# Huber loss over two 8192x8192 matrices: one run of numbers in tiles of 128x13248, four slots, in place of 128x8192 in six

## The chip, the core and the metric

The kernel runs on one core of a Trainium2 chip. The metric is device microseconds of one execution. Three runs of the kernel before took 1873.52, 1872.58 and 1871.90 us; the median, 1872.58, is its time.

## The reference

```python
def reference(pred, target):            # both 8192 x 8192, float32
    delta = 1.0
    diff = pred - target
    abs_diff = np.abs(diff)
    return np.where(abs_diff <= delta, 0.5 * diff**2, delta * (abs_diff - 0.5 * delta))
```

Every output element depends on one element of each input, so any cut of the matrices into tiles will do. The input is 2 x 268.4 MB, the output 268.4 MB: 805.3 MB have to be moved, whatever the order.

The kernels compute the loss as max(|d| - 0.5, 0.5 c^2), where d is the difference and c is d held between bounds. The kernel before holds |d| between 0 and 1; the kernel after holds d between -1 and 1. The square is the same.

## The kernel before

The 8192 rows are cut into 64 tiles of 128 rows by 8192 columns, 4 MB in float32, so a partition holds one row of 32 KB. Six slots of that size lie in on-chip memory. A tile takes two: its pred slot becomes the difference and then its absolute value, and its target slot becomes the clamped value, then the half square, then the output, which is stored from there.

For one tile there are five operations. VectorE subtracts (`sub`, L41), ScalarE takes the absolute value (`absolute`, L49), VectorE clamps (`clamp`, L44), ScalarE squares with a scale (`half_square`, L52), and VectorE adds -0.5 to the absolute value and takes the maximum with the half square (`finish`, L55). The order on each engine is the order in which the program is written, since the schedule is manual. `compute` emits the finish of a tile one tile later, between the subtract and the clamp of the next. The last four tiles are computed in four pieces of 2048 columns each.

All transfers are issued by SyncE (SP) on one queue, in program order. In round i, `load(i)` issues pred (L66) and target (L68) of tile i, then `store` issues the output (L73) of tile i-2. The slots are chosen by lists: `load` takes as the pred slot one whose tile is through with it (`spent`), and as the target slot one whose store has been issued (`free`). So three tiles are asked for before the first store, and a target load waits until the store out of its slot has landed. An SP instruction that waits holds back everything behind it on SP. The target load and the store of the last tile are cut into four pieces of 1 MB.

Of the kernel before, what the change touches and what calls it, by code (L numbers as in the profile page):

```python
# [1 line left out]

# [4 lines left out]


@with_exitstack
def kernel(  # L10
    ctx: ExitStack,
    tc: tile.TileContext,
    pred: bass.AP,
    target: bass.AP,
    out: bass.AP,
):
    nc = tc.nc
    P = 128
    fp32 = mybir.dt.float32
    Alu = mybir.AluOpType  # L20
    Act = mybir.ActivationFunctionType
    SQRT_HALF = 0.70710678118654752

    n_rows, W = pred.shape
    pred_t = pred.rearrange("(n p) m -> n p m", p=P)
    targ_t = target.rearrange("(n p) m -> n p m", p=P)
    out_t = out.rearrange("(n p) m -> n p m", p=P)
    n = pred_t.shape[0]

    NSLOT = 6  # L30
    PIECES = 4
    FINE = 4

    pool = ctx.enter_context(tc.tile_pool(name="slots", bufs=1))
    slots = [pool.tile([P, W], fp32, name=f"slot{k}") for k in range(NSLOT)]
    free = list(range(NSLOT))
    spent = []
    pending = []

    def sub(a, b):  # L40
        nc.vector.tensor_tensor(out=a, in0=a, in1=b, op=Alu.subtract)  # L41

    def clamp(a, b):
        nc.vector.tensor_scalar(  # L44
            out=b, in0=a, scalar1=0.0, scalar2=1.0, op0=Alu.max, op1=Alu.min
        )

    def absolute(a):
        nc.scalar.activation(out=a, in_=a, func=Act.Abs)  # L49

    def half_square(b):
        nc.scalar.activation(out=b, in_=b, func=Act.Square, scale=SQRT_HALF)  # L52

    def finish(a, b):
        nc.vector.scalar_tensor_tensor(  # L55
            out=b, in0=a, scalar=-0.5, in1=b, op0=Alu.add, op1=Alu.max
        )

    def cuts(pieces):
        w = W // pieces  # L60
        return [slice(k * w, (k + 1) * w) for k in range(pieces)]

    def load(i):
        ia = spent.pop(0) if i >= 3 else free.pop(0)
        ib = free.pop(0) if free else spent.pop(0)
        nc.sync.dma_start(out=slots[ia], in_=pred_t[i, :, :])  # L66
        for c in cuts(PIECES if i == n - 1 else 1):
            nc.sync.dma_start(out=slots[ib][:, c], in_=targ_t[i, :, c])  # L68
        return ia, ib

    def store(i, ib):
        for c in cuts(PIECES if i == n - 1 else 1):
            nc.sync.dma_start(out=out_t[i, :, c], in_=slots[ib][:, c])  # L73
        free.append(ib)

    ctx.enter_context(tc.manual_schedule())

    waiting = []

    def settle(keep):  # L80
        while len(waiting) > keep:
            finish(*waiting.pop(0))

    def compute(a, b, pieces):
        lag = 1 if pieces == 1 else 2
        if pieces > 1:
            while waiting and waiting[0][0].shape[1] == W:
                finish(*waiting.pop(0))
        for c in cuts(pieces):
            sub(a[:, c], b[:, c])  # L90
            absolute(a[:, c])
            settle(lag - 1)
            clamp(a[:, c], b[:, c])
            half_square(b[:, c])
            waiting.append((a[:, c], b[:, c]))

    for i in range(n):
        ia, ib = load(i)
        if i >= 2 and i < n - 1:
            store(*pending.pop(0))  # L100
        spent.append(ia)
        pending.append((i, ib))
        compute(slots[ia], slots[ib], PIECES if i >= n - FINE else 1)
    settle(0)
    for p in pending:
        store(*p)


# [1 line left out]
_INS = ['pred', 'target']  # L110
_OUTS = [((8192, 8192), 'float32')]


# [23 lines left out]
```

## Time and profile before

| | |
|---|---|
| median of three runs | 1872.58 us |
| the profiled execution, its own time | 1873.31 us |
| its span in the profile | 1871.5 us |
| VectorE (DVE) busy | 1386.8 us, 74%, 228 instructions |
| ScalarE (ACT) busy | 906.0 us, 48%, 153 instructions |
| moved | 805.36 MB, 430 GB/s over the span |
| loads and stores | 198 transfers on one queue |

The profile is of one execution. The span runs from the first to the last instruction; the execution's own time is 1.8 us longer. Busy shares are means over the span. The DMA row of the page gives, for 40 equal slices, the share of time in which the 16 DMA engines of the core hold a packet, in tenths. A view of windows gives, for each stretch of the span, the busy time and number of instructions of VectorE, ScalarE and GpSimd, then the granted TensorE clock (not used here, 1.00), the DMA share and the GB/s. SPq is SyncE's sequencer, which issues the transfers. "Time to landing" is from the issue of a transfer to the arrival of the last of its 16 completion marks, one from each DMA engine. In the chain of waits, each line gives the start and the duration of a piece, followed back from the last instruction of the program; the lines of a timeline give start, duration, engine, line, operation and shapes, and in brackets how long the engine had been idle and what ended that.

### The profile page before, as it was taken

To read this page: it belongs to the slowest core of one execution; us is meant where nothing else is said; L and a number is where in the kernel's file an instruction comes from. 1 tells how busy PE (TensorE), PEld (TensorE's weight loads), DVE (VectorE), ACT (ScalarE), POOL (GpSimd) and SP (SyncE) were. 2 spreads that over 40 slices of the span, in tenths; PEclk is the share of its full clock that TensorE was granted. 3 is DMA by queue.
4 is the path that set the end of the run, shared out by engine and by line. 5 is a ranking of instruction groups with operands and counts; after the bars stand their busy time and mean duration, and the time that the engine had idled before them with its cause. 6 is when DMAs were issued, how large, how long until landed. Compare 5 with 4: busy or idle time off the path is not lost.

```text
span 1871.5 us, 823 instructions
## 1 busy us (share of the span) xinstructions
DVE 1386.8 (74%) x228; ACT 906.0 (48%) x153; POOL 0.2 (0%) x4
## 2 busy tenths in 40 slices
DVE  3886776868678687686776867768678686686787
ACT  2644545444454444544545445444454444544555
POOL 0000000000000000000000000000000000000000
DMA  9999999999999999999999999999999999999998
GB/s 415 415 432 431 432 432 429 434 426 430 435 431 434 434 431 434 433 432 434 432 432 435 431 434 432 433 434 433 432 433 434 431 435 431 434 433 432 434 434 382
DMA packets 28517, 805.36 MB, mean 430 GB/s; under 512 B 3168, under 2 KB 3168, under 8 KB 3168
## 3 DMA queue, kind: packets, MB, share of 16 engines
q1 hardware_dynamic: 28512, 805.32, 100.0%
q14 instruction: 5, 0.04, 0.0%
HBM read 536.87 MB, written 268.44 MB: 430 GB/s over the span
## 4 chain that ended last, share of the span: by engine, by line
DMA 68%; DVE 31%; ACT 0%; issue 0%; DVEq 0%; SPq 0%
DMA out_dram<-slot 35%; DMA slot<-in_target_dram 32%; DVE slot L41 15%; DVE slot L55 15%; DVE slot L44 1%; ACT slot L49 0%; DVEq L132 0%; DVEq L41 0%; SPq L66 0%; SPq L68 0%; DVEq L44 0%; SPq L73 0%
## 5 line engine op out<-in xcount | busy, mean ns | idle before, releaser
L41 DVE TENSOR_TENSOR slot<-slot,slot 128x8192 f32<-128x8192 f32 (+1 forms) x76 | 558.1, 7343 | 456.2 <-DMA slot<-in_target_dram 456.2
L49 ACT ACTIVATE slot<-slot 128x8192 f32<-128x8192 f32 (+1 forms) x76 | 452.4, 5952 | 576.3 <-DVE slot L41 576.3
L52 ACT ACTIVATE slot<-slot 128x8192 f32<-128x8192 f32 (+1 forms) x76 | 452.3, 5951 | 375.7 <-DVE slot L44 375.7
L55 DVE SCALAR_TENSOR_TENSOR slot<-slot,slot 128x8192 f32<-128x8192 f32 (+1 forms) x76 | 557.5, 7337 | 7.1 <-ACT slot L52 7.1
L44 DVE TENSOR_SCALAR slot<-slot 128x8192 f32<-128x8192 f32 (+1 forms) x76 | 284.8, 3747 | 11.0 <-ACT slot L49 11.0
L49 ACT ACT_TABLE_LOAD x1 | 1.3, 1283 | 0.7 <-PEq L121 0.7
L121 POOL MEMSET const-bfloat16-1.0<- 128x1 bf16 x1 | 0.1, 101 | 0.0
L121 POOL MEMSET const-uint8-127<- 128x1 uint8 x1 | 0.1, 101 | 0.0
L121 POOL MEMSET const-float32-0.0<- 128x1 f32 x1 | 0.1, 98 | 0.2 <-issue 0.2
L121 POOL MEMSET const-float32-1.0<- 128x1 f32 x1 | 0.1, 98 | 0.0
## 6 DMA issues: line engine op xcount, KB each, us to landing
slot<-in_pred_dram SPq DMA_DIRECT2D x64, 4096.0 KB, 30.6
slot<-in_target_dram SPq DMA_DIRECT2D x63, 4096.0 KB, 19.3
out_dram<-slot SPq DMA_DIRECT2D x63, 4096.0 KB, 21.4
slot<-in_target_dram SPq DMA_DIRECT2D x4, 1024.0 KB, 15.2
out_dram<-slot SPq DMA_DIRECT2D x4, 1024.0 KB, 9.8
```

Of the source, the lines that this page charges most:

```text
L41: nc.vector.tensor_tensor(out=a, in0=a, in1=b, op=Alu.subtract)
L44: nc.vector.tensor_scalar(out=b, in0=a, scalar1=0.0, scalar2=1.0, op0=Alu.max, op1=Alu.min)
L49: nc.scalar.activation(out=a, in_=a, func=Act.Abs)
L52: nc.scalar.activation(out=b, in_=b, func=Act.Square, scale=SQRT_HALF)
L55: nc.vector.scalar_tensor_tensor(out=b, in0=a, scalar=-0.5, in1=b, op0=Alu.add, op1=Alu.max)
L121: nc = _bacc.Bacc("TRN2", target_bir_lowering=False, num_devices=1)
```

## The change

The two inputs and the output are each read as one run of 67,108,864 numbers. It is cut into 40 blocks: the first of 128x7616, the other 39 of 128x13248, so a partition holds 52,992 consecutive bytes and rows of the matrices no longer matter. There are four slots in place of six, two for pred (`a0`, `a1`) and two for target and output (`b0`, `b1`); tile i uses the pair i mod 2.

Two tiles are loaded ahead. Then each round computes tile i, stores it, and loads tile i+2. So on SP a store of tile i stands before both loads of tile i+2, and there are 138 transfers in all. Tiles 0 and 1 and the two before the last are loaded in halves, the last in quarters, with its first two pred quarters ahead of its first target quarter. The last store is in three quarters and two eighths.

A tile is computed in thirds of 4416 columns; the first in halves of 3808, the last but one in quarters of 3312 and the last in eighths of 1656. In each piece VectorE subtracts and clamps from -1 to 1, then ScalarE squares and takes the absolute value. The finish of a piece is emitted after the clamp of the third piece from it on; at the end of each tile the rest are emitted, so nothing of a tile is left for the next.

```diff
-    NSLOT = 6
-    PIECES = 4
-    FINE = 4
+    total = pred.shape[0] * pred.shape[1] // P
+    W = 13248
+    H, Q, E = W // 2, W // 4, W // 8
+    widths = [W] * (total // W)
+    if total % W:
+        widths.insert(0, total % W)
+    n = len(widths)
+    starts = [sum(widths[:i]) * P for i in range(n)]
+
+    def block(x, i):
+        flat = x.rearrange("r m -> (r m)")
+        return flat[starts[i] : starts[i] + P * widths[i]].rearrange("(p m) -> p m", p=P)
...
+    a_slots = [pool.tile([P, W], fp32, name=f"a{k}") for k in range(2)]
+    b_slots = [pool.tile([P, W], fp32, name=f"b{k}") for k in range(2)]
...
+    def load(i):
+        a, b = a_slots[i % 2], b_slots[i % 2]
+        def get(dst, src, c):
+            nc.sync.dma_start(out=dst[:, c], in_=block(src, i)[:, c])
+        if i == n - 1:
+            c = cuts([Q] * 4)
+            order = [(0, 0), (0, 1), (1, 0), (1, 1), (0, 2), (1, 2), (0, 3), (1, 3)]
+            for which, k in order:
+                get((a, b)[which], (pred, target)[which], c[k])
+            return
+        w = widths[i]
+        pieces = [w // 2] * 2 if i in (0, 1, n - 3, n - 2) else [w]
+        for c in cuts(pieces):
+            get(a, pred, c)
+            get(b, target, c)
+
+    def store(i):
+        pieces = [Q] * 3 + [E] * 2 if i == n - 1 else [widths[i]]
+        for c in cuts(pieces):
+            nc.sync.dma_start(out=block(out, i)[:, c], in_=b_slots[i % 2][:, c])
+
+    def compute(i):
+        if i == n - 1:
+            pieces = [E] * 8
+        elif i == n - 2:
+            pieces = [Q] * 4
+        elif i == 0:
+            pieces = [widths[0] // 2] * 2
+        else:
+            pieces = [W // 3] * 3
+        todo = []
+        def finish(keep):
+            while len(todo) > keep:
+                a, b = todo.pop(0)
+                nc.vector.scalar_tensor_tensor(                                # L86
+                    out=b, in0=a, scalar=-0.5, in1=b, op0=Alu.add, op1=Alu.max
+                )
+        for c in cuts(pieces):
+            a, b = a_slots[i % 2][:, c], b_slots[i % 2][:, c]
+            nc.vector.tensor_tensor(out=a, in0=a, in1=b, op=Alu.subtract)      # L92
+            nc.vector.tensor_scalar(                                           # L93
+                out=b, in0=a, scalar1=-1.0, scalar2=1.0, op0=Alu.max, op1=Alu.min
+            )
+            nc.scalar.activation(out=b, in_=b, func=Act.Square, scale=SQRT_HALF)
+            nc.scalar.activation(out=a, in_=a, func=Act.Abs)
+            todo.append((a, b))
+            finish(2)
+        finish(0)
...
-    for i in range(n):
-        ia, ib = load(i)
-        if i >= 2 and i < n - 1:
-            store(*pending.pop(0))
-        spent.append(ia)
-        pending.append((i, ib))
-        compute(slots[ia], slots[ib], PIECES if i >= n - FINE else 1)
-    settle(0)
-    for p in pending:
-        store(*p)
+    load(0)
+    load(1)
+    for i in range(n):
+        compute(i)
+        store(i)
+        if i + 2 < n:
+            load(i + 2)
```

More of the change, by code (lines that the diff above doesn't have):

```diff
@@ L22 @@
     SQRT_HALF = 0.70710678118654752
[L24 to L28, printed above, removed]
-    NSLOT = 6
-    PIECES = 4
-    FINE = 4
-    pool = ctx.enter_context(tc.tile_pool(name="slots", bufs=1))
[L35 to L57, printed above, removed]
@@ L59, in cuts @@
-    def cuts(pieces):
-        w = W // pieces
-        return [slice(k * w, (k + 1) * w) for k in range(pieces)]
-    def load(i):
[L64 to L74, printed above, removed]
@@ L76 @@
-    ctx.enter_context(tc.manual_schedule())
[L78 to L95, printed above, removed]
@@ new lines @@
+    starts = [sum(widths[:i]) * P for i in range(n)]
+    def block(x, i):
+        flat = x.rearrange("r m -> (r m)")
+        return flat[starts[i] : starts[i] + P * widths[i]].rearrange("(p m) -> p m", p=P)
+    pool = ctx.enter_context(tc.tile_pool(name="slots", bufs=1))
+    a_slots = [pool.tile([P, W], fp32, name=f"a{k}") for k in range(2)]
+    b_slots = [pool.tile([P, W], fp32, name=f"b{k}") for k in range(2)]
+    def cuts(pieces):
+        at, found = 0, []
+        for w in pieces:
+            found.append(slice(at, at + w))
+            at += w
+        return found
```

## The prediction, as it was written before the result

> **What bounds the kernel now.** I read the head of the page first, then its DMA part, then the trace cut into windows, then the chain of waits, then single instructions.
>
> ```profile
> DVE 1386.8 (74%) x228; ACT 906.0 (48%) x153; POOL 0.2 (0%) x4
> ...
> DMA  9999999999999999999999999999999999999998
> ...
> q1 hardware_dynamic: 28512, 805.32, 100.0%
> ```
>
> No compute engine is full (VectorE 74%). One queue, SP's, carries all 805.3 MB, and its 16 engines hold packets for the whole span. So the time is bytes over rate, plus what is lost at the ends and on the way. I cut the trace into windows of 58.13 us, the time of two tiles in the steady part; the last column is GB/s:
>
> ```profile
> 2.00:60.13 58.13, 30.34 (x5) 21.09 (x4) 0.00 (x0) 1.00 1.00 428
> 60.13:118.26 58.13, 47.49 (x7) 32.19 (x5) 0.00 (x0) 1.00 1.00 417
> ...
> 292.65:350.78 58.13, 43.26 (x6) 27.34 (x5) 0.00 (x0) 1.00 1.00 430
> 350.78:408.91 58.13, 43.26 (x6) 27.09 (x5) 0.00 (x0) 1.00 1.00 430
> ...
> 990.21:1048.34 58.13, 43.32 (x7) 28.12 (x4) 0.00 (x0) 1.00 1.00 433
> ...
> 1864.00:1871.50 7.50, 0.00 (x0) 0.00 (x0) 0.00 (x0) 1.00 0.41 172
> ```
>
> The steady rate is 433.0 GB/s (six transfers of 4.194 MB in 58.13 us), and 805.3 MB at it are 1859.8 us. The span is 11.7 us longer, and that is all that a better order can win: 2.6 us before the first bytes flow at full rate; 2.1 us in 60 to 118, where the first stores begin ((433 - 417)/433 x 58.13); some 1.7 us between 234 and 467, at 0.4 us per window of 430; the rest, near 5 us, at the end, where the 16 DMA engines stop one after another and the last landing is waited for. That the engines drift apart is in the trace's completion marks, sixteen to a transfer: 0.4 us apart for the first transfer, 0.6 at 92 us, 2.3 at 308, 5.2 at 504, and 5.2 still for the last but few. The slowest engine sets the end.
>
> The chain of waits, one round of two tiles:
>
> ```profile
> 1626.18 21.36 DMA out_dram<-slot
> 1647.55 19.34 DMA slot<-in_target_dram
> 1666.94 0.04 issue
> 1666.98 8.69 DVE slot L41
> 1675.68 8.61 DVE slot L55
> ```
>
> It goes through VectorE, but it adds up to 58.1 us, the DMA time of two tiles: the 21.36 and 19.34 us are queueing behind other transfers (one alone needs 9.69). VectorE is on it by default; shortening it wins nothing.
>
> **The change, part by part.** I work from this one execution: span 1871.5, 1873.31 with 1.8 us around it; the median of the three runs, 1872.58, lies 0.73 us below that.
>
> *Bytes*: the same 805.3 MB, to the same places in order. Nothing won.
>
> *Fewer, larger transfers*: before there are 198 (64 + 63 + 63 of 4 MB, eight of 1 MB); after, 138 in SP's order, most of 128x13248, 6.783 MB. Each moves 128 rows, eight to a DMA engine. Price of one transfer more: in the tail the last full load lands at 1831.6 and the four 1 MB loads behind it at 1834.1, 1836.5, 1839.0 and 1841.5 (issue time plus time to landing). 4 MB in four pieces take 9.9 us, against 9.69 in one; four store pieces take 9.72 to 9.8, against 9.66. So three transfers more cost 0.06 to 0.2 us, 0.02 to 0.06 each. Sixty fewer win 1.2 to 3.6 us; I take the middle, **-2.4**. If rows of 53 KB were split in two on the way, this could be nothing.
>
> The Trainium skill speaks against more ("DMA: Bandwidth & Descriptors", "Where 436 GB/s comes from"): sixteen ports give 435.2 GB/s at most. The trace agrees: 433.0 is 99.5% of it. By that figure the bytes alone are 1850.4 us, so no order of transfers could come below that plus the ends.
>
> *Start*: before, three tiles (25.2 MB) are asked for at once and run out at about 60.7 us; the first store is issued at 60.14, in the nick of time, and the queue runs nearly dry (about 0.3 us). After, tiles 0 and 1 (7.8 and 13.6 MB) run out at 2.6 + 18.0 + 31.3 = 52 us. Tile 0 lands in halves at 11.6 and 20.6. Durations at the new widths are on the line through the 8192 and 2048 rows:
>
> ```profile
> 64.36 8.69 DVE L41 TENSOR_TENSOR slot<-slot,slot 128x8192 f32<-128x8192 f32 x1
> 64.48 7.03 ACT L52 ACTIVATE slot<-slot 128x8192 f32<-128x8192 f32 x1 [5.91 <-DVE slot L44]
> 81.57 4.42 DVE L44 TENSOR_SCALAR slot<-slot 128x8192 f32<-128x8192 f32 x1
> ...
> 1814.53 2.28 DVE L55 SCALAR_TENSOR_TENSOR slot<-slot,slot 128x2048 f32<-128x2048 f32 x1
> 1814.65 1.91 ACT L49 ACTIVATE slot<-slot 128x2048 f32<-128x2048 f32 x1 [6.19 <-DVE slot L41]
> 1816.73 1.22 DVE L44 TENSOR_SCALAR slot<-slot 128x2048 f32<-128x2048 f32 x1
> ```
>
> So two-input VectorE operations take 2.28 + 1.043 ns per column over 2048: 4.1 us at 3808, 4.75 at 4416; the clamp 2.1 and 2.46; ScalarE 3.4 and 3.88. Behind the second half of tile 0: subtract 24.7, clamp 26.9, Square and Abs 33.7, finish 37.8. Store 0 is issued 14 us before the queue is dry: **-0.3**.
>
> *Steady part, the new wait*: there are two pairs of slots in place of six single ones. SP issues store i, then load i+2. Store i waits on VectorE at the head of SP; behind it stand only the loads of i+2, which need the same slots, so nothing else is held up. From the landing of tile i's last load to the issue of store i, VectorE runs nine operations, 3 x (4.75 + 2.46 + 4.75) = 35.9 us; ScalarE's last Abs ends at about 30.5, before the last finish starts at 31.1. In that time the queue holds store i-1, both loads of i+1: 3 x 6.783 MB / 433 = 47.0 us. Slack 11 us, some 9 after issue latency (0.73 to about 2 us at the start). The target load of i+2 also waits for store i to land; the pred load, 15.7 us, covers it (before: 9.7). Cost: nothing, hidden behind 47 us of transfers. If the path came to 47 us, every us more would cost about 38.
>
> *Clamp from -1, and Square before Abs*: the clamp no longer waits for ScalarE (before, L44 waits 11.0 us in all); same instruction. It shortens the path already counted. Nothing.
>
> *End*: the last three tiles come in halves and quarters. Behind the last load stand stores 38 and 39, 31.4 us; the last eighths need some 12 us of VectorE. Before the same holds (last load 1841.5, last store issued 1861.2, 9.4 to landing). Nothing; the pieces are counted in the 138.
>
> *Turns from loads to stores*: the slow windows are early, and the first is where stores begin. 40 stores of tiles take the place of 64. If each turn costs as before and all matter, the 1.7 us and the lag of the last engine shrink to 40/64; if a fixed number of turns is needed until the engines stand apart, nothing is won; if each costs in proportion to its transfer (13248/8192 = 1.62), nothing either, and more if it lasts. Bounds: -4 (most of the 2.1, the 1.7 and some of the lag gone) to +13 (below). I take **-0.8**, the middle of "by count" (-1.7) and "no change", nearest to the rows.
>
> One rule of the skill bears on this and nothing here shows it: the same page ("Latency and other measured facts") tells of rates falling when rows lie large powers of two apart, from 512 KiB up; rows go from 32 KB to 52,992 bytes apart. The trace's 433 leaves it almost nothing to mend.
>
> Sum: 1871.5 - 2.4 - 0.3 - 0.8 = 1868.0 span, 1869.8 with its surroundings, less 0.73: 1869.1 as a median. The bounds of the transfer price move it by 1.2; as the slow windows end by themselves before a third of the run, I lean half a us low: **1868.5 us**, -0.22%. A measurement of this kernel can tell about 0.2% (3.7 us) from no change, so this forecast sits on that line.
>
> **Rivals.**
> 1. *Turns become cheap* (E): early windows run at 433. Then 2.1 + 1.7 us and part of the lag go as well: 1862 to 1866. For: the loss ends by itself at 467, so it isn't needed. Against: the first turns still find all engines in step.
> 2. *Nothing gained* (B): rows split, or turns costing as much or somewhat more: 1870.5 to 1876. For: the queue is already full.
> 3. *Slower, turns that never settle* (C): each of 40 turns costs 0.2 us as in the 430 windows (0.4 per two tiles), or 0.33 if it goes with the transfer: 8 to 13 us in place of 1.7, so 1876 to 1881. It decides from 0.2 us per turn through the whole run. For: four windows in a row show it. Against: 22 windows after 467 don't.
> 4. *Slower, starvation* (D): path of 36 us over 47. Idle before stores; at 1 us over, 1906. Against: every duration is measured, 9 us of slack.
>
> **How the numbers follow.** Forecast (1866 to 1870.5) 50%, of it 28 below 1868.8 and 22 above; E 20; B 18; C 9; D 3. Faster 0.48, same 0.40, slower 0.12. The range, 1863 to 1876, leaves out C, D and some 8 of E's 20.
>
> **What would show it.** The windows after 500 us should show 433 to 434 GB/s. L92, L93 and L86 at 4.75, 2.46 and 4.75 us. SP's waits for VectorE before stores end some 9 to 11 us before the queue is dry, and no DMA slice falls below 9. VectorE 74%. Wrong if windows in the middle show 430 or less (C), if idle DMA stands before stores (D), or if packets of half a row appear (B).

## The result, and the profile after

| | before | after |
|---|---|---|
| median, same chip | 1872.97 us (13 runs, 1871.81 to 1876.33) | 1868.56 us (13 runs, 1867.82 to 1869.17) |
| ratio | | 0.9975, 95% interval 0.9966 to 0.9983 |
| span of the profiled execution | 1871.5 us | 1867.4 us |
| last landing in it | 1870.6 us | 1866.5 us |

The change wins 4.4 us, 0.25%, and the times of the kernel after lie closer together. The page of the kernel after, its engines, its DMA share in 40 slices, and its queue (packets, MB, share of 16 engines):

```profile
DVE 1406.2 (75%) x375; ACT 903.9 (48%) x251; POOL 0.2 (0%) x4
...
DMA  9999999999999999999999999999999999999999
...
q1 hardware_dynamic: 19872, 805.32, 99.9%
```

The picture is the same: VectorE at three quarters, the queue full. What differs is the number of packets, 19,872 against 28,512. Taking away the 16 marks of each transfer (138 x 16, 198 x 16), 17,664 data packets are left against 25,344: exactly 128 to a transfer, so a row of 53 KB goes as one packet. The windows of the kernel after, with GB/s last:

```profile
2.00:60.13 58.13, 34.27 (x10) 20.95 (x7) 0.00 (x0) 1.00 1.00 423
60.13:118.26 58.13, 45.45 (x13) 31.56 (x9) 0.00 (x0) 1.00 1.01 431
234.00:467.00 233.00, 177.40 (x45) 113.75 (x30) 0.00 (x0) 1.00 1.00 433
600.00:1700.00 1100.00, 824.70 (x210) 523.24 (x138) 0.00 (x0) 1.00 1.00 434
1859.00:1867.40 8.40, 0.00 (x0) 0.00 (x0) 0.00 (x0) 1.00 0.52 214
```

The kernel before, over two of these stretches:

```profile
234.00:467.00 233.00, 172.19 (x24) 109.71 (x16) 0.00 (x0) 1.00 1.00 430
600.00:1700.00 1100.00, 817.46 (x115) 534.26 (x76) 0.00 (x0) 1.00 1.00 433
```

The gain is in two places. In the steady part the rate is higher. The last column rounds it; a straight line through the bytes moved between 600 and 1700 us gives 432.8 GB/s before and 433.6 after, and 805.3 MB at these are 1860.6 and 1857.3 us: 3.3 us of the 4.1 by which the last landings differ. In the early part the slow stretch from 60 to 467 us is gone (417 and 430 before, 431 and 433 after), less what the kernel after loses sooner, before 60 us (423 against 428).

One round of two tiles in the chain of waits of the kernel after (start, duration, what):

```profile
931.02 26.90 DMA out_dram<-b
957.92 0.02 issue
957.94 31.24 DMA b<-in_target_dram
989.17 0.03 issue
989.20 0.02 DVEq L92
989.22 0.04 issue
989.27 4.77 DVE a L92
994.04 0.02 issue
994.06 2.46 DVE b L93
...
1010.85 14.02 DVE b L86 x3
1024.86 0.02 issue
1024.88 26.91 DMA out_dram<-b
```

From the landing at 989.17 to the issue of the store at 1024.88 are 35.7 us, as worked out (35.9), and from store to store 93.86 us, the DMA time of two tiles: 40.70 MB at 433.6.

### The profile page after: what moved, and what is told of

It is laid out like the page before. It is cut to its first block, busy times and chain, and to the rows that moved or that the text cites. A ratio compares the mean times of both kernels' runs of the same rounds, so it can differ in the third digit from the quotient of the medians.

```text
span 1867.4 us, 994 instructions
## 1 busy us (share of the span) xinstructions
DVE 1406.2 (75%) x375; ACT 903.9 (48%) x251; POOL 0.2 (0%) x4
## 3 DMA queue, kind: packets, MB, share of 16 engines
q1 hardware_dynamic: 19872, 805.32, 99.9%
## 4 chain that ended last, share of the span: by engine, by line
DMA 61%; DVE 37%; issue 0%; SPq 0%; DVEq 0%
DMA b<-in_target_dram 33%; DMA out_dram<-b 28%; DVE b L86 15%; DVE a L92 15%; DVE b L93 8%; SPq L53 0%; DVEq L136 0%; DVEq L92 0%
## 5 line engine op out<-in xcount | busy, mean ns | idle before, releaser
L96 ACT ACTIVATE b<-b 128x4416 f32<-128x4416 f32 (+3 forms) x125 | 461.1, 3688 | 945.6 <-DVE b L93 945.6
L92 DVE TENSOR_TENSOR a<-a,b 128x4416 f32<-128x4416 f32 (+3 forms) x125 | 565.4, 4523 | 439.2 <-DMA b<-in_target_dram 439.2
L86 DVE SCALAR_TENSOR_TENSOR b<-a,b 128x4416 f32<-128x4416 f32 (+3 forms) x125 | 558.6, 4521 | 2.7 <-ACT a L97 2.7
L97 ACT ACTIVATE a<-a 128x4416 f32<-128x4416 f32 (+3 forms) x125 | 460.3, 3682 | 0.0
L93 DVE TENSOR_SCALAR b<-a 128x4416 f32<-128x4416 f32 (+3 forms) x125 | 293.1, 2344 | 4.3
```

What stands on the lines that cost most here:

```text
L86: nc.vector.scalar_tensor_tensor(out=b, in0=a, scalar=-0.5, in1=b, op0=Alu.add, op1=Alu.max)
L93: nc.vector.tensor_scalar(out=b, in0=a, scalar1=-1.0, scalar2=1.0, op0=Alu.max, op1=Alu.min)
```

## The experiments

Twelve runs, in three groups; each was timed beside the kernel before on its chip (medians there 1873.4 to 1873.75). My theory going in: the gain is a price per transfer, sixty fewer of them, and the rest is the early turns from loads to stores. The rivals: the new order and the cut ends win; the row pitch wins (32 KB before); the number of turns from loads to stores counts by itself.

**Both kernels again**, as anchors.

> The changed kernel again, as an anchor on the same chip as the next three: 1868.6 us, 0.25% below the kernel before.

Measured: 1868.50 us (9 runs, ratio 0.9972, 0.9963 to 0.9982), as before.

> The kernel before once more, for a second profile: if its slow windows are its own, 60 to 118 us shows 417 GB/s again and some window between 234 and 467 shows 430; if they were of that one execution, they sit elsewhere.

Measured: one execution, 1877.31 us, span 1875.5. Its windows:

```profile
60.13:118.26 58.13, 47.44 (x7) 32.06 (x5) 0.00 (x0) 1.00 0.99 415
234.00:467.00 233.00, 171.57 (x24) 110.43 (x16) 0.00 (x0) 1.00 1.00 427
600.00:1700.00 1100.00, 817.36 (x114) 534.25 (x76) 0.00 (x0) 1.00 1.00 433
```

So the slow early stretch belongs to the kernel before, and its size changes from one execution to the next: here 4 us more than in the first profile, with the same 433 afterwards. It ends at about 583 us here, at 467 there. Between 118 and 600 us the first profile falls 1.7 us behind a steady 433.0 GB/s and this one 6.1; the two profiles of the kernel after fall behind by 0.4 and 0.1 (1.0 and 0.8, measured against their own 433.6). Two profiles of each kernel don't prove it, but this would explain why the times before spread over 4.5 us and those after over 1.4.

**Packets or transfers.** First, each whole transfer in two:

```diff
-        pieces = [w // 2] * 2 if i in (0, 1, n - 3, n - 2) else [w]
+        pieces = [w // 2] * 2
...
-        pieces = [Q] * 3 + [E] * 2 if i == n - 1 else [widths[i]]
+        pieces = [Q] * 3 + [E] * 2 if i == n - 1 else [widths[i] // 2] * 2
```

> The changed kernel with every transfer of a whole tile cut into two halves of its columns: 247 transfers in place of 138, each of 8 rows per DMA engine, half as long; tiles, computation and the 40 turns from loads to stores as in the changed kernel. Theory: 109 x 0.037 to 0.05 = 4.0 to 5.5 us more, 1872.6 to 1874.1. Rival turns (only the number of turns from loads to stores counts): 1868.6. Rival order: 1868.6.

Measured: 1875.91 us, ratio 1.0013 (1.0004 to 1.0022) to the kernel before, 7.4 above the kernel after: the sign of the theory, and more than its price.

Then the same number of transfers as in the kernel after, but with a gap in the middle of each row of a slot, so that a row goes as two packets:

```diff
-    a_slots = [pool.tile([P, W], fp32, name=f"a{k}") for k in range(2)]
+    a_slots = [pool.tile([P, 2, H + 16], fp32, name=f"a{k}") for k in range(2)]
...
+    def part(slot, i, c):
+        h = widths[i] // 2
+        if c.start == 0 and c.stop == widths[i]:
+            return slot[:, :, 0:h]
...
+    def runs(x, i, c):
+        h = widths[i] // 2
+        if c.start == 0 and c.stop == widths[i]:
+            return block(x, i).rearrange("p (t m) -> p t m", t=2)
...
-            nc.sync.dma_start(out=dst[:, c], in_=block(src, i)[:, c])
+            nc.sync.dma_start(out=part(dst, i, c), in_=runs(src, i, c))
```

The target slots and the stores are changed in the same way, and a third of a tile is now a third of each half. VectorE's operations on it take the same 4.75 and 2.46 us.

> The changed kernel, 138 transfers, but each slot row is two runs of 6624 numbers with a gap of 64 bytes, so a whole transfer has 16 packets of 26 KB per DMA engine in place of 8 of 53 KB. Price of a packet: if the 0.037 to 0.05 us are all per packet, this costs as much as cutting the transfers in two, about 4 to 5 us: 1872.6 to 1873.6. If they are per transfer, nothing: 1868.6.

Measured: 1875.21 us, ratio 1.0009 (1.0000 to 1.0018), 6.7 above the kernel after. The queue of the halved transfers, then that of the split rows, and a window of each:

```profile
q1 hardware_dynamic: 35568, 805.32, 100.0%
...
600.00:1700.00 1100.00, 824.54 (x209) 533.41 (x140) 0.00 (x0) 1.00 1.00 432
```

```profile
q1 hardware_dynamic: 33824, 805.32, 100.1%
...
600.00:1700.00 1100.00, 820.45 (x209) 523.27 (x138) 0.00 (x0) 1.00 1.00 432
```

Both have 31,616 data packets (35,568 less 247 x 16; 33,824 less 138 x 16), one with 109 transfers more than the other, and both run at 431.9 GB/s by the line through the bytes. So the price goes by packets, not by transfers. To each DMA engine it is 1104 packets after, 1584 before, 1976 here; 805.3 MB take 1857.3, 1860.6 and 1864.6 us at the three rates. That is 7 ns per packet from after to before, and 8 ns from after to here. A hundred transfers more or less, with the same packets, are 0.7 us by the medians, and the intervals of the two runs overlap. The lengths of the packets themselves agree: their medians between 600 and 1700 us are 982 ns for 26,496 bytes, 1213 for 32,768 and 1956 for 52,992. A line through the three is 8 ns for each packet plus its bytes at 27.2 GB/s on each engine, 435.3 on all sixteen.

**Smaller tiles**, in the order of the kernel after:

```diff
-    W = 13248
+    W = 8192        # 8128 and 6624 in the other two
...
-            pieces = [W // 3] * 3
+            pieces = [W // 4] * 4      # thirds as they were at 6624
```

> The changed kernel with tiles of 128x8192 (64 tiles, 210 transfers, rows of 32 KB as before; computed in quarters), its own slots, order and ends. Theory (each transfer costs 0.037 to 0.05 us, so fewer transfers win): 72 more than in the changed kernel, 1868.6 + 2.7 to 3.6 = 1871.3 to 1872.2, level with the kernel before. Rival order (the four slots, the early first store and the cut ends win, not the size): 1868.6. Rival row pitch (32 KB apart is what hurts): about 1872 here, but see the next run.

> The same with 128x8128: 64 tiles and a first of 4096, 213 transfers, rows 32,512 bytes apart, no power of two. Theory: as 128x8192 within 0.5 us, 1871.4 to 1872.4. Rival row pitch: 1868.6 to 1869, 3 us below 128x8192.

> The changed kernel with tiles of 128x6624: 80 tiles, 258 transfers of the size of the halved ones, 80 turns from loads to stores in place of 40. Theory of transfers alone: 120 x 0.037 to 0.05 = 4.4 to 6 us more, 1873.0 to 1874.6, that is 0.5 above the halved transfers. With turns of some 0.05 us each besides: 2 us above the halved transfers. Rival order: 1868.6.

Measured: 1898.77, 1898.34 and 1906.78 us, ratios 1.0133 (1.0119 to 1.0147), 1.0128 (1.0113 to 1.0144) and 1.0181 (1.0164 to 1.0197). No theory had this: 30 and 38 us above the kernel after, where packets explain some 5 and 7. The pitch rival falls (8128 and 8192 within 0.4 us), and so does the order rival, since this order alone is 25 us slower than the kernel before at the same tile.

Most of the loss sits in the steady part, where nothing else happens: by the bytes moved, 20 of the 30 us and 23 of the 38 lie between 600 and 1700 us. 128x8192, then 128x6624:

```profile
1000.00:1700.00 700.00, 532.84 (x284) 341.82 (x188) 0.00 (x0) 1.00 1.00 426
```

```profile
600.00:1700.00 1100.00, 835.29 (x413) 535.56 (x275) 0.00 (x0) 1.00 1.00 424
```

The completion marks gave a hint. Two issues of a store, at 128x8192 and in the kernel after (start, duration):

```profile
1010.13 0.34 SPq L70 DMA_DIRECT2D out_dram<-b  x1
```

```profile
1024.88 0.34 SPq L70 DMA_DIRECT2D out_dram<-b  x1
```

At 128x8192 a store is issued at 1010.13 us; the last DMA engine finishes the load in front of it at 1017.05, but the first one at 1012.15. The engines that are ahead have 2 us of work left when the store is issued. In the kernel after, the store is issued at 1024.88, the first engine finishes the load in front of it at 1032.60, the last at 1036.12: 7.7 us left for the first. So I formed another theory: a store must come before the *first* of the sixteen engines runs out, and the margin is the slack less the lead of that engine over the last one.

**The slack, taken away and given back.** Full tiles in halves lengthen the path with the same transfers:

```diff
-            pieces = [W // 3] * 3
+            pieces = [W // 2] * 2
```

> The changed kernel with full tiles computed in halves in place of thirds. The path from the last load's landing to the store is then 7.05 + 3.6 + 7.05 + 3.6 on VectorE, the two ScalarE operations of the second half to 33.7, and a finish: 40.8 us in place of 36, under 47.0 less some 2 us of issue. Theory of slack: no change, 1868.6 within 0.5. Rival (the slot loop is already at its limit, every us of path shows in every tile): 5 x 38 = 190 us more.

Measured: 1880.52 us, ratio 1.0041 (1.0029 to 1.0054): neither. Two stretches of it, and the issues of SP (start, duration):

```profile
96.00:471.60 375.60, 281.46 (x48) 180.51 (x32) 0.00 (x0) 1.00 1.00 433
1000.00:1700.00 700.00, 522.45 (x89) 338.45 (x60) 0.00 (x0) 1.00 1.00 429
```

```profile
1032.39 0.34 SPq L70 DMA_DIRECT2D out_dram<-b  x1
1032.83 0.38 SPq L53 DMA_DIRECT2D a<-in_pred_dram  x1
1055.27 0.33 SPq L53 DMA_DIRECT2D b<-in_target_dram  x1
1080.08 0.34 SPq L70 DMA_DIRECT2D out_dram<-b  x1
```

The slack by the last engine is 6.4 to 7.6 us from 182 us on (at 1032.39 it is 7.2: the last mark of the load in front comes at 1039.57). At 324 us the marks lie 2.9 us apart, the first engine has 3.5 us left, and the rate is 433. Past 1000 us they lie some 5.2 apart, the first engine has 1.0 to 2.2 us left, and rounds of 47.4 to 48.2 us appear among those of 46.9. In these rounds packets around the turns, of many engines, take 0.1 to 0.9 us longer than their usual 1.96; in the kernel after, between 985 and 1095 us, not one takes 0.02 longer. So the same path costs nothing until the engines have drifted apart.

The other kernels fit. Between 600 and 1700 us the first engine has 0.7 to 2.3 us left at the stores of 128x8192, and 1.1 to 1.9 at those of 128x6624, at 426 and 424 GB/s. It has 7.0 to 7.9 in the kernel after; in the kernel before, whose marks lie 5.2 apart too, it has 6.4 at the stores and 4.4 at the target loads, which wait for a landing. One part of my theory does not hold: in none of these runs does the first engine run out. The halves lose 9.4 us on the kernel after in this stretch, and their packets are longer by 9.1 us per engine. So a short reserve makes packets at the turns longer; why it does so stays open.

At the other end, one piece per tile:

```diff
-            pieces = [W // 3] * 3
+            pieces = [W]
```

> The changed kernel with full tiles computed in one piece: path from landing to store 13.96 + 7.0 + 11.2 + 11.2 + 13.96 = 57.4 us, against 47.0 us of queued transfers. Theory of the slot loop: about 10.4 + 2 us of idle DMA in each of some 37 tiles, 1868.5 + 460 = 2330 us (2250 to 2400). Rival (other transfers fill in): under 1950.

Measured: 2261.86 us (one run). From store to store:

```profile
1029.31 0.34 SPq L70 DMA_DIRECT2D out_dram<-b  x1
...
1086.68 0.34 SPq L70 DMA_DIRECT2D out_dram<-b  x1
```

57.37 us per tile, the path alone; the 2 us of issue that I added aren't paid, since the next tile has landed by then. The path is 10.4 us over the 47 of the queued transfers, and that costs 393 us, 38 for each us over, as the prediction had it. Here the engines do run out, in every round, and their marks lie only some 0.5 us apart.

Then tiles of 8192 with three pairs of slots, so a whole tile more stands in the queue (29 us):

```diff
-    a_slots = [pool.tile([P, W], fp32, name=f"a{k}") for k in range(2)]
+    a_slots = [pool.tile([P, W], fp32, name=f"a{k}") for k in range(3)]     # b too; i % 3
...
+    load(2)
...
-        if i + 2 < n:
-            load(i + 2)
+        if i + 3 < n:
+            load(i + 3)
```

> The run of 128x8192 tiles with three pairs of slots in place of two and three tiles loaded ahead; order, ends and 210 transfers as there. If that run lost its 30 us because a store was issued only about 7 us before the queue was dry, so that the DMA engines that were ahead ran out, a tile more in the queue (29 us) cures it, and what remains is the price of packets: 576 more per DMA engine than in the changed kernel at 7.7 to 8.4 ns, 1868.5 + 4.4 to 4.8 = 1873 (within 1). Rival (many turns from loads to stores cost by themselves, 64 against 40): stays near 1898.

> The same with 128x8128, rows 32,512 bytes apart. Theory: as 128x8192 in three pairs, 1873 within 1. Rival row pitch (power of two): 2 to 3 us below it.

Measured: 1879.87 and 1881.83 us, ratios 1.0030 (1.0020 to 1.0041) and 1.0037 (1.0025 to 1.0050). 19 us of the 30 are back, with the same number of turns, packets and transfers, and the pitch rival falls again, as 8128 is 2 us the slower; but 7 us are missing from the forecast. Two stretches at 128x8192:

```profile
600.00:1700.00 1100.00, 851.24 (x453) 547.77 (x301) 0.00 (x0) 1.00 1.00 433
...
1745.00:1860.00 115.00, 94.71 (x62) 60.04 (x41) 0.00 (x0) 1.00 0.98 404
```

The steady part is cured. The missing time is in the last 130 us (404, against 428 in this stretch of the kernel after: 6.4 us), where loads are cut. There a target piece waits for a store to land, and the pred piece that covers the wait is only half as long: the target half is issued at 1763.93 us (below), when the first engine has finished the pred half in front at 1762.48. It looks like the same fault at another wait, this time with the first engine out of work; I didn't test it apart.

```profile
1763.93 0.33 SPq L53 DMA_DIRECT2D b<-in_target_dram  x1
```

**The cut ends.**

```diff
-        if i == n - 1:
+        if False:
             c = cuts([Q] * 4)
...
-        pieces = [w // 2] * 2 if i in (0, 1, n - 3, n - 2) else [w]
+        pieces = [w]
```

> The changed kernel without the cut loads: every tile is loaded whole, the last too (124 transfers); stores and computation as they were. At the start tile 0 is computed later, store 0 at about 42 us, still before the queue is dry at 52: nothing, or -0.5 us for 14 fewer transfers. At the end the last tile can be computed only when it has all landed: 36 us of VectorE from there, against 31.4 us of stores still to move. Theory: +6 to +9 us, 1874.6 to 1877.6. Rival (the pieces at the end hide nothing, as stores stand in the queue anyway): 1868.

Measured: 1880.35 us, ratio 1.0036 (1.0023 to 1.0050), 11.9 above the kernel after. Its end:

```profile
1840.00:1879.00 39.00, 31.58 (x21) 21.76 (x15) 0.00 (x0) 1.00 0.55 231
```

The last store of a whole tile has landed at 1850.1 us, and from there the stores of the last tile go out one by one, as VectorE hands them over, the last issued at 1871.8. The start is no slower: up to 118 us as many bytes have moved as in the kernel after. So the cut loads at the end are worth 12 us, more than I expected; without them the change would lose.

## Why the prediction was right, point by point

The median came out at 1868.56 us against a forecast of 1868.5. That it is so near is partly luck. The first term was 0.9 us too small, and the half us that I leaned low, for the slow windows, made up for most of it. Start and turns together won 1.1 us, as forecast, but neither part was the one I gave.

- **What bounds it**: right. The DMA rate and the ends set the time in all runs but the one-piece one.
- **Fewer, larger transfers, -2.4 (1.2 to 3.6)**: the mechanism is right in kind, its unit is wrong, its size a little low. The four tail pieces from which I took it have four times the packets as well as four times the transfers, and I charged the transfers. It is 7 to 8 ns per packet and engine: 480 fewer won 3.3 us. Rows were not split.
- **The ceiling of the Trainium skill** ("DMA: Bandwidth & Descriptors", "Where 436 GB/s comes from"): holds. 433.6 is the highest steady rate of any kernel here, against 435.2; single slices of a page read 436, with lower ones beside them.
- **Start, -0.3**: the size is wrong. Store 0 is issued at 38.8 us, 14 before the first engine is through with the loads in front, as worked out. Yet the kernel after loses 0.8 us at 50 to 56, where loads turn to store 0 with all engines in step. A store in good time does not make the first turn free. From 2 to 118 us together it still wins 0.6.
- **Turns, -0.8 (bounds -4 to +13)**: right in sign. In the first pair of profiles it is about -0.5 after 118 us, once the rate is taken out, and against the second profile of the kernel before it would be near -5, past my bound of -4. I gave one value to what differs by execution.
- **Steady part, nothing**: right in outcome, and wrong in the safety that I claimed. The path is 35.7 us and the slack 11.2. But I weighed the slack against the last engine alone and took the lead of the others as harmless: rival D, "path of 36 us over 47", was to begin at 47. The halves showed that 4.8 us more of path cost 12 us in all, at a slack of 6.4 to 7.6. There was no loss with 3.4 us or more left for the first engine, and a clear one with 1.0 to 2.2. The kernel after has 7.7 there.
- **End, nothing**: right for the change as it is; the experiment without the cuts shows that it hung on them.
- **Rival C**, turns that never settle: did not happen in the kernel after (434 GB/s from 600 to 1700), but did in the smaller tiles and in the halves, with the short reserve told of above. Why turns are dear while the engines are in step, and why the early stretch of the kernel before is dearer and longer than that of the kernel after, stays open: the tile, the lookahead and the number of turns all differ. The pitch of the rows the skill's page warned of ("DMA: Bandwidth & Descriptors", "Latency and other measured facts") is from 512 KiB up; at 32 KB leaving the power of two won nothing, twice.

## What to carry to other kernels

In a kernel that is full of transfers, count packets, not transfers: a longer row per partition is the gain, and it is small (7 to 8 ns a packet). With two slots the queue's reserve is the tile's transfer time less its computation, so it grows with the tile; measure it against the first of the sixteen engines to finish, not the last. In these runs 3 us and more were enough, and 2 or less were not. Cut the last loads finely and leave the rest whole.

## What the runs showed of the hardware

The sixteen DMA engines of one queue do not stay together. In the kernels before and after, their marks for one transfer lie 0.3 to 0.6 us apart at the first transfers and 3.5 to 5.3 us in the steady part, and the lead stays to the end; in the one-piece run, where the queue runs dry in every round, they lie 0.5 apart. A turn from loads to stores costs a packet of each engine up to 1.1 us while they are in step (the first store of the kernel before, 58 to 70 us), and next to nothing once they stand apart with work queued (between 600 and 1700 us, 21 of 9003 packets of the kernel after are more than 0.1 us over their usual 1.96).
